# First stage of a hybrid decoder block: eighteen column tiles in the quarter passes instead of twelve, and three of eight modulation groups on VectorE

## The chip, the cores and the metric

One core of a Trainium2 chip runs the whole program. The metric is device microseconds per execution, the median of the runs shown. The engines are TensorE (PE, with its weight loads as PEld), VectorE (DVE), ScalarE (ACT), GpSimd (POOL) and SyncE (SP, which here only issues DMAs). Each works through its own instructions in the order in which they were written.

## The reference

A decoder block for 256 tokens of width 2048. Only its first part concerns the change:

```python
c_act = jax.nn.silu(c)
mod = jnp.einsum("bd,de->be", c_act, w_ada[l]) + b_ada[l]
shift1, scale1, gate1, shift2, scale2, gate2 = jnp.split(mod[:, None, :], 6, axis=-1)
h = rms_norm(x, norm1_g) * (1.0 + scale1) + shift1
proj = jnp.einsum("bsd,de->bse", h, w_in)      # 2048 -> 9248 columns
```

`proj` is cut into a gate branch and a recurrent branch (RG-LRU), and into the z, x, B, C and dt columns of an SSD (Mamba-2) branch with a causal convolution and a chunked scan. An output projection, a second normalization with modulation and a retrieval mixer (PEER) follow. All inputs are float32. The reference works in float32; the kernel splits each float32 weight and activation into a high and a low part and adds three products (high x high, high x low, low x high).

## The kernel before

**Column tiles.** `w_in` is stored as 73 column tiles of 128 columns, in the order `ETILES` names them: 0 to 15 are the LRU gate, 16 to 31 the LRU x, 32 to 47 z, 48 to 63 the SSD x, 64 to 67 B, 68 to 71 C, and 72 is dt. A tile's product with `hT` (the normalized, modulated input, 16 blocks of 128 rows, each with a high and a low part) ends in a PSUM bank, and `evac` takes it from there: for a convolved tile one ACT operation, three DVE taps, a tanh and two POOL or one DVE operation; for dt a softplus and two scans, a chain of some twenty small DVE operations spread over the following steps.

**Weight items.** Weights come in items of 512 KB through four `raw` buffers. ACT copies an item into the high part of an `hl` tile (L144, four of these), DVE subtracts it for the low part (L153), and then the next item's DMA is issued on SP.

**First stage.** The modulation of one quarter of `h`'s rows needs eight groups (`ada_group`), each of which reads 1 MB of `w_ada` (two `adw` tiles out of eleven): groups 0 to 3 of a quarter give the scale, 4 to 7 the shift. A group is four PE matmuls (L257) with the activated `c` as weights, four partial rows in one bank. After four groups `ada_row` copies the rows (ACT, L266), sums and turns them into columns on PE (L271) and finishes on DVE (L278, L280). Then ACT and DVE write that quarter of `hT` (L286, L288).

The eight groups of the first quarter run alone. Then come the passes 0, 1 and 2: in pass q, `w_pass` multiplies that quarter of the rows with each of the first twelve tiles, two tiles (a pair, 24 matmuls, L319 to L322) to an item, and the eight groups for the next quarter stand between the pairs. The sums of the six pairs stay in banks 0 to 5. Pass 3 has no groups; each tile goes to `evac` there. After each half of a pair or slot `mid` runs the steps that were put off (`defer`).

**Slots.** The other 61 tiles follow one by one in slots, two items each, 48 or 32 matmuls (L812 to L814, or the wide form in L444 and L446), into banks 0 to 2 in turn. Each slot also takes one step from the list `bg` (`bg_pop`): first an empty one, then the transposes of the dt results (L492, `cols_pe`), then for each of the four SSD groups the transposes of its x (L528, `a_pe`), the products of B and C, and so on. A group's steps are put on the list when its last x tile has been handed to `evac` (51 for the first group). `ada_step` accumulates the other modulation rows on DVE (L384), `ADA_SSD` of them per slot.

The order of the work is the order of the code; `manual_schedule` moves nothing.

Of the kernel before, what the change touches and what calls it, by code (L numbers as in the profile page):

```python
# [27 lines left out]
NRAW = 4  # L28
NHL = 4
GD = 3  # L30
ADA_SSD, ADA_LRU, ADA_OUT = 0.65, 1.1, 0.74

N0 = 12
NQ = 4
NG = 8
ETILES = [72]
for _g in range(4):
    ETILES += [64 + _g, 32 + 4 * _g, 68 + _g, 48 + 4 * _g, 33 + 4 * _g, 49 + 4 * _g, 50 + 4 * _g,
               34 + 4 * _g, 51 + 4 * _g, 35 + 4 * _g]
ETILES += [3, 16, 17, 18, 19, 20, 21, 22, 4, 5, 6, 7, 23]  # L40
for _g in range(2, 4):
    ETILES += [4 * _g + _i for _i in range(4)] + [16 + 4 * _g + _i for _i in range(4)]
for _n, _p in enumerate((3, 5, 7)):
    ETILES.insert(_p, _n)

KORDER = list(range(16, 32)) + list(range(16))

# [11 lines left out]
def hybrid_kernel(ctx, tc, xT, cols, w_ada, w_in, lru_w, w_o1, w_o2, w_q, keys, u_t, v_t, fng, out):  # L59
# [11 lines left out]
    def bank(n):  # L71
        return psum.tile([128, 512], FT, name=f"b{n}")
# [177 lines left out]
    def ada_group(n):  # L250
        q, r = divmod(n, 8)
        sec, c4 = divmod(r, 4)
        if c4 == 0:
            aw["b"] = bank(6 + sec)
        w = [ar.pop(2 * n + i) for i in range(2)]
        for g in range(4):
            pe.matmul(aw["b"][32 * g:32 * g + 32, :], cz[:, 4 * c4 + g, :], w[g // 2][:, g % 2],  # L257
                      start=(c4 == 0), stop=(c4 == 3), skip_group_check=True)
        for i in range(2):
            ada_load(2 * n + 11 + i)  # L260
        if c4 == 3:
            defer(lambda b=aw["b"]: ada_row(q, sec, b))

    def ada_row(q, sec, b):
        a = arow[:, sec]
        act.activation(a, b, AF.Copy)  # L266

        def cols_pe():
            p = bank(6 + sec)
            for i in range(4):  # L270
                pe.matmul(p[:, i:i + 1], a[:, i * 128:(i + 1) * 128], ones[:, 0:1], start=True, stop=True)  # L271
            defer(lambda: ada_fin(q, sec, p))
        defer(cols_pe)
# [33 lines left out]
    hT = keep.tile([128, 16, 2, 256], FR, name="H")  # L307
    b0 = {}

    def w_pass(q, n, done=None, late=False):  # L310
        w = take()
        for i in range(2):
            e = 2 * n + i
            if q == 0 and i == 0:
                b0[n] = bank(n)
            ps = b0[n][:, i * 256:(i + 1) * 256]
            for kk in range(4):
                k, c = 4 * q + kk, slice(i * 512 + kk * 128, i * 512 + (kk + 1) * 128)
                pe.matmul(ps, w[:, 0, c], hT[:, k, 0, :], start=(k == 0 and i == 0), stop=False,  # L319
                          skip_group_check=True)  # L320
                pe.matmul(ps, w[:, 0, c], hT[:, k, 1, :], start=False, stop=False, skip_group_check=True)
                pe.matmul(ps, w[:, 1, c], hT[:, k, 0, :], start=False, stop=(k == 15), skip_group_check=True)  # L322
# [20 lines left out]
    for q in range(3):
        for n, gs in enumerate(((0, 1), (2,), (3, 4), (5,), (6, 7))):
            w_pass(q, n)
            for g in gs:
                ada_group(8 * (q + 1) + g)
        mid()
        w_pass(q, n2 - 1, late=True)
# [169 lines left out]
    def ssd_steps(g):  # L519
# [117 lines left out]
        def seq(*fs):  # L637
            def go():
                for f in fs:
# [961 lines left out]
```

## Time and profile before

| | us |
|---|---|
| median of 3 runs (lowest to highest) | 2157.16 (2155.39 to 2159.13) |
| the profiled execution | 2172.81 |
| its span, first to last instruction | 2171.1 |
| PE busy / DVE / ACT / POOL | 2089.6 / 1397.3 / 960.7 / 879.2 |

An instruction's row gives its start in the span, its duration, engine, line, operation, and the tiles as out<-in; a bracket tells how long the engine was idle before it and what ended that. A row by line gives the busy time and the mean in ns. In rows by stage each engine's busy time is followed by its number of instructions. PE's matmuls overlap, so start to start tells more than a duration.

### The profile page before, as it was taken

Reading aid. Unit: us, or ns where it says so; the run is one execution under the profiler, and the core shown is the slowest. Engines: PE = TensorE matmul, PEld = TensorE weight load, DVE = VectorE, ACT = ScalarE, POOL = GpSimd, SP = SyncE. Lnnn points to the kernel's source line nnn. Section 1 sums busy time; section 2 is a strip of 40 time slices with the busy share of each in tenths; the row PEclk is TensorE's granted clock in tenths of the full one; section 3 lists DMA queues with packets and bytes.
Section 4 is the critical chain, followed back from the end, with each engine's and each line's share of the span. In section 5 each row is a group of like instructions: output and inputs, shape, how many; then the busy total and the mean of one; then the engine's idle time right before and its main releaser. Section 6 shows DMA issues by size and latency. Waiting matters only on the chain.

```text
span 2171.1 us, 34830 instructions
## 1 busy us (share of the span) xinstructions
PE 2089.6 (96%) x13092; PEld 1639.8 (76%) x13092; DVE 1397.3 (64%) x1996; ACT 960.7 (44%) x1470; POOL 879.2 (40%) x729
## 2 busy tenths in 40 slices
PE   7999999999999989999999999999999989999996
PEld 4779999978999888888788778666666656656663
DVE  2368887978878868879979996334334344344344
ACT  3346665666644454444345554333333333333332
POOL 0013233312212010001415561677777757767774
PEclk9999999999999999999999999999999999999998
DMA  9966566767789954568677778799999999999996
GB/s 372 387 233 223 195 207 216 235 224 251 262 295 322 334 176 166 191 220 282 229 255 238 247 247 288 270 367 346 347 343 354 347 325 346 373 345 348 358 356 234
DMA packets 248264, 616.33 MB, mean 284 GB/s; under 512 B 37752, under 2 KB 121864, under 8 KB 225800
## 3 DMA queue, kind: packets, MB, share of 16 engines
q1 hardware_dynamic: 188944, 387.73, 51.9%
q0 software_dynamic: 45056, 175.52, 21.9%
q10 hardware_dynamic: 14096, 50.86, 6.9%
q8 instruction: 103, 1.69, 0.3%
q14 instruction: 65, 0.53, 0.1%
HBM read 692.41 MB, written 14.69 MB: 326 GB/s over the span
## 4 chain that ended last, share of the span: by engine, by line
PE 70%; DVE 14%; DMA 9%; issue 4%; ACT 2%; POOL 0%; SPq 0%; another core or an unknown queue 0%; DVEq 0%; POOLq 0%; ACTq 0%
PE b L444 13%; PE b L1439 12%; PE b L1353 10%; PE b L446 7%; DVE hl L153 6%; PE b L1281 3%; PE b L1279 3%; PE b L1280 3%; PE b L918 3%; DMA raw<-in_w_in 2%; DMA two<-in_w_ada 2%; DMA adw<-in_w_ada 2%; PE b L812 2%; PE b L813 2%; PE b L814 2%
## 5 line engine op out<-in xcount | busy, mean ns | idle before, releaser
L144 ACT ACTIVATE hl<-raw 128x1024 fp32r<-128x1024 f32 x594 | 628.6, 1060 | 1072.2 <-PE b L1439 192.7
L153 DVE TENSOR_TENSOR hl<-raw,hl 128x1024 fp32r<-128x1024 f32 x594 | 766.5, 1301 | 140.2 <-ACT hl L144 121.0
L444 PE MATMUL b<-H,hl 128*128 128x512 f32 x1376 | 494.2, 402 | 3.2 <-DVE qT L450 2.8
L446 PE MATMUL b<-H,hl 128*128 128x256 f32 x1376 | 386.6, 281 | 5.2 <-DVE hl L153 5.1
L444 PEld LDWEIGHTS b<-H,hl 128*128 128x128 f32 x1376 | 259.1, 188 | 89.9 <-issue 20.2
L1332 POOL DMA_INDIRECT X<-ad,X x256 | 289.5, 1131 | 87.9 <-issue 76.8
L1439 PE MATMUL b<-hl,X 128*128 128x512 f32 x1152 | 279.0, 400 | 11.8 <-issue 10.0
L1439 PEld LDWEIGHTS b<-hl,X 128*128 128x128 f32 x1152 | 216.6, 191 | 87.0 <-issue 39.4
L446 PEld LDWEIGHTS b<-H,hl 128*128 128x128 f32 x1376 | 260.5, 189 | 7.4 <-DVE hl L153 6.6
L1281 PE MATMUL b<-hl,H 128*128 128x512 f32 x640 | 249.9, 390 | 4.0 <-DVE hl L153 3.7
L1279 PE MATMUL b<-hl,H 128*128 128x512 f32 x640 | 252.7, 395 | 0.0
L1280 PE MATMUL b<-hl,H 128*128 128x512 f32 x640 | 249.4, 390 | 0.0
L1323 POOL DMA_INDIRECT vq<-in_v_t,X x128 | 151.5, 1184 | 114.5 <-PE b L1353 38.1
L1323 POOL DMA_INDIRECT tk<-in_v_t,X x128 | 144.0, 1125 | 71.2 <-PE b L1353 31.4
L814 PE MATMUL b<-H,hl 128*128 128x256 f32 x560 | 160.0, 286 | 4.2 <-DVE hl L153 4.2
L1343 DVE TENSOR_TENSOR Wz<-X 128x4 f32<-128x4 f32 x64 | 11.0, 172 | 236.3 <-DMA X<-ad,X 123.0
L812 PE MATMUL b<-H,hl 128*128 128x256 f32 x560 | 162.4, 290 | 0.0
L813 PE MATMUL b<-H,hl 128*128 128x256 f32 x560 | 159.7, 285 | 0.0
L1281 PEld LDWEIGHTS b<-hl,H 128*128 128x128 f32 x640 | 120.1, 188 | 31.7 <-DVE hl L153 6.8
L384 DVE SCALAR_TENSOR_TENSOR adacc<-adr,cact,adacc 128x1024 f32<-128x1024 f32 x90 | 127.7, 1419 | 21.9 <-DMA adr<-in_w_ada 21.8
L1279 PEld LDWEIGHTS b<-hl,H 128*128 128x128 f32 x640 | 120.1, 188 | 23.9
L1280 PEld LDWEIGHTS b<-hl,H 128*128 128x128 f32 x640 | 120.3, 188 | 23.7
(323 smaller groups left out, 3212.2 us busy)
## 6 DMA issues: line engine op xcount, KB each, us to landing
raw<-in_u_t SPq DMA_DIRECT2D x208, 512.0 KB
raw<-in_w_in SPq DMA_DIRECT2D x146, 512.0 KB
adr<-in_w_ada SPq DMA_DIRECT2D x96, 512.0 KB
adw<-in_w_ada SPq DMA_DIRECT2D x64, 512.0 KB
raw<-in_w_o SPq DMA_DIRECT2D x64, 512.0 KB
raw<-in_u_t ACTq DMA_DIRECT2D x48, 512.0 KB
raw<-in_v_t SPq DMA_DIRECT2D x48, 512.0 KB
raw<-in_v_t ACTq DMA_DIRECT2D x48, 512.0 KB
```

Source lines behind the costliest of these rows:

```text
L144: act.activation(t[:, 0], r, AF.Copy)
L153: dve.tensor_sub(t[:, 1], r, t[:, 0].bitcast(FT))
L444: pe.matmul(ps, w[:, 0, c], x[:, k].rearrange("p a b -> p (a b)"), start=(k == 0), stop=False, skip_group_check=True)
L446: pe.matmul(ps[:, :256], w[:, 1, c], x[:, k, 0], start=False, stop=(k == 15), skip_group_check=True)
L812: pe.matmul(ps, wh, hT[:, k, 0, :], start=(k == 0), stop=False)
L1279: pe.matmul(o, hh, w[:, 0, :, kk], start=(k == 0), stop=False)
L1280: pe.matmul(o, hl_, w[:, 0, :, kk], start=False, stop=False)
L1281: pe.matmul(o, hh, w[:, 1, :, kk], start=False, stop=(k == 15))
L1323: pool.indirect_dma_start(x, None, vf, bass.IndirectOffsetOnAxis(ap=eV[:, t:t + 1], axis=0), bounds_check=E1 - 1, oob_is_err=False)
L1332: pool.indirect_dma_start(wA[:, n:n + 1], None, adf, bass.IndirectOffsetOnAxis(ap=eW[:, t:t + 1], axis=0), bounds_check=T * E1 - 1, oob_is ...
L1353: pe.matmul(sb[c][32 * g:32 * g + 32, :], Wz[:, x:x + 32], vs[4 * (q % 2) + g][:, c * 512:(c + 1) * 512], start=(m == 0), stop=(m == 31), ...
L1439: pe.matmul(ob[tb * 2 + c], w[:, i, s], v[:, k, c * 512:(c + 1) * 512], start=(jj == 0 and (i, k) == (0, 0)), stop=(jj == JD - 1 and k == 1))
```

## The change

The first eighteen tiles (nine pairs) are now computed in the passes. Pairs 0 to 5 keep banks 0 to 5. Pairs 6, 7 and 8 share bank 6 in turn; when one of them leaves the bank, its partial sum is copied (ACT) or added (DVE) into the first half of `xx`, which is free by then, and in pass 3 DVE adds it back to the bank before `evac` reads it (`first_evac`). Pass 0 holds eight pairs, pass 1 ten (pair 8 with two quarters), pass 2 nine, pass 3 nine. Of the eight groups of a quarter, 0, 4 and 5 run on DVE as four operations each into `arow`; the five others stay on PE, in bank 7, and DVE adds the two (L297 in the new file, in place of ACT's copy). In pass 3 `bg_pop` runs after each of the pairs 6, 7 and 8, and the empty first step of the SSD groups is left out except for the fourth. The order of the tiles behind the first twelve is rearranged, `y_ssd` (which takes `xx`'s place) is allocated later, and `ADA_SSD` is 0.86 instead of 0.65.

```diff
-ADA_SSD, ADA_LRU, ADA_OUT = 0.65, 1.1, 0.74
-N0 = 12
+ADA_SSD, ADA_LRU, ADA_OUT = 0.86, 1.1, 0.74
+N0 = 18
+NP = 6
+PASSES = [["P0", "G0", "G1", "P1", "G2", "P2", "G3", "P6", "P3", "G4", "P4", "G5", "G6", "P5", "G7", "P7"],
+          ["P0", "G0", "G1", "P6", "P1", "G2", "P2", "G3", "P8", "P8", "G4", "P3", "G5", "P4", "G6", "P5", "G7", "P7"],
+          ["P0", "G0", "G1", "P6", "P1", "G2", "P2", "G3", "P8", "P3", "G4", "P4", "G5", "G6", "P5", "G7", "P7"],
+          [f"P{_n}" for _n in range(N0 // 2)]]
...
+ADA_DVE = (0, 4, 5)
+ETILES = [72, 64, 32, 0, 68, 1, 48, 2, 33, 49, 50, 34, 51, 35, 3, 65, 36, 37, 69, 52, 38, 53, 54, 39, 55]
+for _g in range(2, 4):
...
     def ada_group(n):
...
-        if c4 == 0:
-            aw["b"] = bank(6 + sec)
...
-        for g in range(4):
-            pe.matmul(aw["b"][32 * g:32 * g + 32, :], cz[:, 4 * c4 + g, :], w[g // 2][:, g % 2],
-                      start=(c4 == 0), stop=(c4 == 3), skip_group_check=True)
+        if r in ADA_DVE:
+            a = arow[:, sec]
+            for g in range(4):
+                c, x = cact[:, 4 * c4 + g:4 * c4 + g + 1], w[g // 2][:, g % 2]
+                if c4 == 0 and g == 0:
+                    dve.tensor_scalar(a, x, c, None, op0=OP.mult)
+                else:
+                    dve.scalar_tensor_tensor(a, x, c, a, op0=OP.mult, op1=OP.add)
+        else:
+            first = r - 1 in ADA_DVE
+            if first:
+                aw["b"] = bank(7)
+            for g in range(4):
+                pe.matmul(aw["b"][32 * g:32 * g + 32, :], cz[:, 4 * c4 + g, :], w[g // 2][:, g % 2],
+                          start=first, stop=(c4 == 3), skip_group_check=True)
...
     def ada_row(q, sec, b):
         a = arow[:, sec]
-        act.activation(a, b, AF.Copy)
+        dve.tensor_add(a, b, a)
 
         def cols_pe():
-            p = bank(6 + sec)
+            p = bank(7)
...
+    def part(n):
+        j = 2 * (n - NP)
+        return xx[:, 0, j:j + 2, :].rearrange("p a b -> p (a b)")
+
-    def w_pass(q, n, done=None, late=False):
+    def w_pass(q, n, first, last, done=None, late=False):
         w = take()
+        if first:
+            b0[n] = bank(n if n < NP else n - NP if done else NP)
...
+        if last and not done:
+            def save(b=b, o=part(n), add=n in saved):
+                if add:
+                    dve.tensor_add(o, b, o)
+                else:
+                    act.activation(o, b, AF.Copy)
+            saved.add(n)
+            defer(save)
...
-        bg.extend([(None, None, 0), (a_pe, a_ew, 0),
+        if g == 3:
+            bg.append((None, None, 0))
+        bg.extend([(a_pe, a_ew, 0),
...
-    for n in range(n2):
-        w_pass(3, n, lambda e, ps: defer(lambda: evac(ETILES[e], ps)))
+
+    def first_evac(e, ps):
+        n, i = divmod(e, 2)
+        if n >= NP:
+            dve.tensor_add(ps, part(n)[:, i * 256:(i + 1) * 256], ps)
+        evac(ETILES[e], ps)
+    for q, n in passes[3]:
+        w_pass(q, n, n >= NP, True, lambda e, ps: defer(lambda: first_evac(e, ps)))
+        if n >= NP:
+            bg_pop()
...
-        ada["bank"] = 6 if slot >= 44 else (slot + 2) % 3
+        ada["bank"] = 6 if slot >= 38 else (slot + 2) % 3
```

The first of three places: DVE's order at the start, before and after. `xx` is the normalized input, `X` the row `arow`, `adw` a tile of `w_ada`. Before:

```order
L303 RECIPROCAL rstd_142<-rstd_142 128x256
L305 TENSOR_TENSOR xx<-xx,rstd_142 128x2048 x2
L278 TENSOR_TENSOR mod<-b_199,cc 128x4
L280 SCALAR_TENSOR_TENSOR mod<-mod,cc 128x4
L278 TENSOR_TENSOR mod<-b_237,cc 128x4
L288 SCALAR_TENSOR_TENSOR H<-xx,mod,H 128x256 x4
```

After:

```order
L334 RECIPROCAL rstd_142<-rstd_142 128x256
L336 TENSOR_TENSOR xx<-xx,rstd_142 128x2048 x2
L280 TENSOR_SCALAR X_95<-adw,cact 128x512
L282 SCALAR_TENSOR_TENSOR X_95<-adw,cact,X_95 128x512 x3
L297 TENSOR_TENSOR X_95<-b_156,X_95 128x512
L280 TENSOR_SCALAR X_95<-adw,cact 128x512
L282 SCALAR_TENSOR_TENSOR X_95<-adw,cact,X_95 128x512 x7
L309 TENSOR_TENSOR mod<-b_198,cc 128x4
L311 SCALAR_TENSOR_TENSOR mod<-mod,cc 128x4
L297 TENSOR_TENSOR X_95<-b_217,X_95 128x512
L309 TENSOR_TENSOR mod<-b_237,cc 128x4
L319 SCALAR_TENSOR_TENSOR H<-xx,mod,H 128x256 x4
```

Group 0's four operations and groups 4 and 5 now stand on DVE behind the two multiplications of `xx` and ahead of the scale's and the shift's last steps.

The second: DVE in pass 3, around the end of the dt chain (`dtt`, `acsr`) and the evacuation of tile 51. Before:

```order
L153 TENSOR_TENSOR hl<-raw,hl 128x1024
L482 TENSOR_TENSOR acsr<-dtt_1096,acsr 128x256
L421 SCALAR_TENSOR_TENSOR X_72<-b_492,hcw,X_72 128x255
L421 SCALAR_TENSOR_TENSOR X_72<-b_492,hcw,X_72 128x254
L421 SCALAR_TENSOR_TENSOR X_72<-b_492,hcw,X_72 128x253
L153 TENSOR_TENSOR hl<-raw,hl 128x1024
L486 TENSOR_TENSOR dtt_1097<-dtt_1097 128x128
L434 SCALAR_TENSOR_TENSOR X_72<-stmp,b_492 128x256
```

After:

```order
L531 TENSOR_TENSOR acsr<-dtt_1372,acsr 128x256
L470 SCALAR_TENSOR_TENSOR X_72<-b_514,hcw,X_72 128x255
L470 SCALAR_TENSOR_TENSOR X_72<-b_514,hcw,X_72 128x254
L470 SCALAR_TENSOR_TENSOR X_72<-b_514,hcw,X_72 128x253
L174 TENSOR_TENSOR hl<-raw,hl 128x1024
L535 TENSOR_TENSOR dtt_1373<-dtt_1373 128x128
L483 SCALAR_TENSOR_TENSOR X_72<-stmp,b_514 128x256
L851 TENSOR_TENSOR b_1581<-xx,b_1581 128x256
L470 SCALAR_TENSOR_TENSOR X_72<-b_1581,hcw,X_72 128x255
```

The chain's last operation (L486, now L535) had ten splits between the last quarter's H and itself and has nine; behind it, `b_1581` is the bank of pair 6, to which DVE adds the kept sum (L851) before tile 51's taps.

The third: PE around the transposes of dt (`dtt`) and of the first SSD group's x. Before, dt's stand between the second slot (bank `b_1376`) and the third:

```order
L444 MATMUL b_1376<-H,hl 128x512
L446 MATMUL b_1376<-H,hl 128x256
L492 MATMUL b_1425<-ident,dtt_1096 128x32 x2
L492 MATMUL b_1425<-ident,dtt_1097 128x32 x3
L812 MATMUL b_1431<-H,hl 128x256
```

After, between the pairs 7 (`b_1625`) and 8 (`b_1672`):

```order
L356 MATMUL b_1625<-H,hl 128x256
L357 MATMUL b_1625<-H,hl 128x256
L541 MATMUL b_1666<-ident,dtt_1372 128x32 x2
L541 MATMUL b_1666<-ident,dtt_1373 128x32 x3
L354 MATMUL b_1672<-H,hl 128x256
```

The x transposes stood between the fourth slot (`b_1502`) and the fifth:

```order
L444 MATMUL b_1502<-H,hl 128x512
L446 MATMUL b_1502<-H,hl 128x256
L528 MATMUL b_1552<-ident,X_72 128x128 x4
L528 MATMUL b_1557<-ident,X_72 128x128 x4
L812 MATMUL b_1562<-H,hl 128x256
```

and stand after the change between pair 8 and the first slot (`b_1725`):

```order
L356 MATMUL b_1672<-H,hl 128x256
L357 MATMUL b_1672<-H,hl 128x256
L577 MATMUL b_1715<-ident,X_72 128x128 x4
L577 MATMUL b_1720<-ident,X_72 128x128 x4
L872 MATMUL b_1725<-H,hl 128x256
```

Between pair 5 and dt's transposes stood two slots and now stand two pairs, which are half as long; up to x's it was four slots and is three pairs.

More of the change, by code (lines that the diff above doesn't have):

```diff
@@ L30, with pass_items @@
 GD = 3
-ADA_SSD, ADA_LRU, ADA_OUT = 0.65, 1.1, 0.74
-N0 = 12
+ADA_SSD, ADA_LRU, ADA_OUT = 0.86, 1.1, 0.74
[5 more added lines that the diff above has]
+          [f"P{_n}" for _n in range(N0 // 2)]]
+def pass_items():
+    done = [0] * (N0 // 2)
+    for p in PASSES:
+        o = []
+        for x in p:
+            n = int(x[1])
+            if x[0] == "P":
+                o.append((done[n], n))
+                done[n] += 1
+            else:
+                o.append((None, n))
+        yield o
 NQ = 4
 NG = 8
-ETILES = [72]
-for _g in range(4):
+ADA_DVE = (0, 4, 5)
+ETILES = [72, 64, 32, 0, 68, 1, 48, 2, 33, 49, 50, 34, 51, 35, 3, 65, 36, 37, 69, 52, 38, 53, 54, 39, 55]
+for _g in range(2, 4):
     ETILES += [64 + _g, 32 + 4 * _g, 68 + _g, 48 + 4 * _g, 33 + 4 * _g, 49 + 4 * _g, 50 + 4 * _g,
                34 + 4 * _g, 51 + 4 * _g, 35 + 4 * _g]
-ETILES += [3, 16, 17, 18, 19, 20, 21, 22, 4, 5, 6, 7, 23]
+ETILES += [16, 17, 18, 19, 20, 21, 22, 4, 5, 6, 7, 23]
 for _g in range(2, 4):
     ETILES += [4 * _g + _i for _i in range(4)] + [16 + 4 * _g + _i for _i in range(4)]
-for _n, _p in enumerate((3, 5, 7)):
-    ETILES.insert(_p, _n)
 KORDER = list(range(16, 32)) + list(range(16))
@@ L102, in hybrid_kernel @@
     items = []
-    for q in range(4):
-        for n in range(0, N0, 2):
-            items.append(w_in[n:n + 2, :, q * 512:(q + 1) * 512].rearrange("e p c -> p e c"))
+    for p in pass_items():
+        for q, n in p:
+            if q is not None:
+                items.append(w_in[2 * n:2 * n + 2, :, q * 512:(q + 1) * 512].rearrange("e p c -> p e c"))
     for n in range(N0, NE):
@@ L308, in hybrid_kernel @@
     b0 = {}
-    def w_pass(q, n, done=None, late=False):
+    def part(n):
+        j = 2 * (n - NP)
+        return xx[:, 0, j:j + 2, :].rearrange("p a b -> p (a b)")
+    def w_pass(q, n, first, last, done=None, late=False):
         w = take()
+        if first:
+            b0[n] = bank(n if n < NP else n - NP if done else NP)
+        b = b0[n]
         for i in range(2):
[L313 to L316, printed above, removed]
+            ps = b[:, i * 256:(i + 1) * 256]
             for kk in range(4):
                 k, c = 4 * q + kk, slice(i * 512 + kk * 128, i * 512 + (kk + 1) * 128)
-                pe.matmul(ps, w[:, 0, c], hT[:, k, 0, :], start=(k == 0 and i == 0), stop=False,
+                pe.matmul(ps, w[:, 0, c], hT[:, k, 0, :], start=(first and kk == 0 and i == 0), stop=False,
                           skip_group_check=True)
                 pe.matmul(ps, w[:, 0, c], hT[:, k, 1, :], start=False, stop=False, skip_group_check=True)
-                pe.matmul(ps, w[:, 1, c], hT[:, k, 0, :], start=False, stop=(k == 15), skip_group_check=True)
+                pe.matmul(ps, w[:, 1, c], hT[:, k, 0, :], start=False, stop=(last and kk == 3),
+                          skip_group_check=True)
             if i and not late:
@@ L326, in w_pass @@
             if done:
-                done(e, ps)
+                done(2 * n + i, ps)
+        if last and not done:
+            def save(b=b, o=part(n), add=n in saved):
+                if add:
+                    dve.tensor_add(o, b, o)
+                else:
+                    act.activation(o, b, AF.Copy)
+            saved.add(n)
+            defer(save)
         if late:
             issue_split()
-    n2 = N0 // 2
+    saved = set()
     for n in range(8):
@@ L342, in hybrid_kernel @@
         issue_split()
[L343 to L349, printed above, removed]
+    passes = list(pass_items())
+    for p in range(3):
+        for j, (q, n) in enumerate(passes[p]):
+            if q is None:
+                ada_group(8 * (p + 1) + n)
+            elif n < NP:
+                w_pass(q, n, q == 0, False)
+            else:
+                at = [x for x in passes[p] if x[0] is not None and x[1] == n]
+                if j == len(passes[p]) - 1:
+                    mid()
+                w_pass(q, n, (q, n) == at[0], (q, n) == at[-1], late=j == len(passes[p]) - 1)
         while any(stages):
@@ L620, in i_ew @@
         def i_ew():
+            nonlocal y_ssd
+            if y_ssd is None:
+                y_ssd = mix.tile([128, 16, 2, 256], FR, name="yssd", tag="Y1")
             sq = Z["sq"]
@@ L734, in evac @@
     def evac(e, ps):
-        nonlocal y_ssd
         if e == 72:
-            y_ssd = mix.tile([128, 16, 2, 256], FR, name="yssd", tag="Y1")
             S["BCs"] = mix.tile([128, 2, 2, 256], FT, name="BCs", tag=L[6])
```

## The prediction

> **What bounds the kernel now.** I read the page first, then the busy times by stage, then the order of time on TensorE (PE), VectorE (DVE) and the DMA queue around the change, then the waits.
>
> ```profile
> span 2171.1 us, 34830 instructions
> PE 2089.6 (96%) x13092; PEld 1639.8 (76%) x13092; DVE 1397.3 (64%) x1996; ACT 960.7 (44%) x1470; POOL 879.2 (40%) x729
> ```
>
> PE is busy nearly throughout, so work taken off it counts wherever PE is also what ends last. By stage (columns: PE, weight load, DVE, ACT, POOL, granted clock, DMA share, GB/s):
>
> ```profile
> 39.10:71.30 32.20, 30.04 (x219) 22.72 (x220) 7.95 (x11) 10.06 (x16) 0.00 (x0) 0.92 1.05 387
> 71.30:101.05 29.75, 29.19 (x230) 22.46 (x229) 9.28 (x14) 10.65 (x17) 0.00 (x0) 0.96 1.05 386
> 101.05:129.40 28.35, 28.02 (x227) 21.16 (x226) 9.27 (x14) 10.63 (x17) 0.00 (x0) 1.00 0.94 345
> 129.40:146.76 17.36, 17.36 (x146) 17.36 (x145) 16.94 (x31) 10.71 (x19) 2.07 (x3) 1.00 0.62 215
> 146.76:175.50 28.74, 25.05 (x174) 22.57 (x173) 27.85 (x46) 15.15 (x26) 9.63 (x10) 1.00 0.54 180
> 249.00:317.00 68.00, 66.85 (x499) 61.96 (x498) 60.74 (x96) 41.56 (x76) 22.48 (x19) 1.00 0.63 204
> ```
>
> The rows start where PE takes up passes 0, 1, 2 and 3 and the first slot. The first three are the passes 0 to 2: DMA at 386 GB/s and PE are both full, DVE is idle two thirds of the time. Rows four and five are pass 3 and the first slots: there DVE is the full engine (16.94 of 17.36, 27.85 of 28.74). The last row is one group of ten slots with its SSD steps: DVE at 89%. So the change adds DVE work where DVE is free, but sends PE into pass 3, where DVE is behind.
>
> **Parts that cancel.** Nine pair quarters (three pairs, three passes) move from the slots to the passes. A pair is 24 matmuls; the fourth row holds 144 in 17.36 us, 2.9 us a pair, so +26.0. Two slots run between these rows:
>
> ```profile
> 286.17 0.39 PE L812 MATMUL b<-H,hl 128*128 128x256 f32 x1
> ...
> 297.68 0.59 PE L612 MATMUL b<-sqv,ones 128*128 128x256 f32 x2
> ```
>
> That is 5.76 us a slot; six tiles lose three quarters of theirs: -25.9. Where both are bound by PE the move is worth nothing.
>
> **Groups off PE: -7.8.** A pass before has three places with two groups in a row and two with one:
>
> ```profile
> 104.11 1.92 PE L257 MATMUL b<-adw,cz 128*32 128x512 f32 x16
> 105.97 0.39 PE L319 MATMUL b<-H,hl 128*128 128x256 f32 x1
> ...
> 109.03 1.07 PE L257 MATMUL b<-adw,cz 128*32 128x512 f32 x8
> 110.02 0.38 PE L319 MATMUL b<-H,hl 128*128 128x256 f32 x1
> ```
>
> Two take 1.86 us from start to start, one 0.99: 3 x 1.86 + 2 x 0.99 = 7.56. After, five single ones remain, 4.95; -2.6 a pass, three passes. Their twelve DVE operations a pass, about 0.72 us each (half of L384 below), are 9 us in some 35 of a DVE with 9 us of other work: hidden.
>
> **The start: +4.0.** Group 0 moves behind the two multiplications L305 in DVE's order, and the queue on SP waits for it, since load 11 goes into group 0's first tile.
>
> ```profile
> 19.45 4.49 DVE L305 TENSOR_TENSOR xx<-xx,rstd 128x2048 f32<-128x2048 f32 x2
> 18.08 3.62 SPq L248 DMA_DIRECT2D adw<-in_w_ada  x6
> 22.42 5.09 SPq L136 DMA_DIRECT2D raw<-in_w_in  x4
> 27.89 0.37 SPq L248 DMA_DIRECT2D adw<-in_w_ada  x1
> 32.05 1.05 PE L257 MATMUL b<-adw,cz 128*32 128x512 f32 x4 [1.78 <-DMA adw<-in_w_ada]
> L384 DVE SCALAR_TENSOR_TENSOR adacc<-adr,cact,adacc 128x1024 f32<-128x1024 f32 x90 | 127.7, 1419 | 21.9 <-DMA adr<-in_w_ada 21.8
> ```
>
> Before, load 11 is issued at 18.08. After, DVE ends L305 at 23.94 and frees the first tile two operations later, at about 25.2. Loads follow each other every 1.37 us ((27.89 - 22.42) / 4). What was issued ahead, 8.1 MB at 387 GB/s from 2.2 us on, has landed by about 23.5, so the DMA engines run dry for 1.7 us, and load 11 then pays a whole latency. It lands near 29 instead of 25: all that follows is 4.0 late, and PE's last group of the first eight waits for such a load (32.05). Bounds: 1.7 (the dry time alone) and 7.1 (the issue's delay); 4.0 lies between, by latency.
>
> **Waits within the passes: -2.4.** Passes 0 to 2 take 90.3 us; three at the undisturbed 27.8 would take 83.3, so 7.0 are waits and half clock:
>
> ```profile
> PE b L271 <- ACT X L266: 3.0, 4, 1.7
> PE b L322 <- DVE hl L153: 1.8, 1, 1.8
> 36.30:43.10 6.80, 5.05 (x20) 4.52 (x21) 6.15 (x8) 3.93 (x6) 0.00 (x0) 0.50 1.05 387
> 70.40:73.80 3.40, 3.40 (x18) 3.40 (x18) 3.02 (x6) 1.54 (x4) 0.00 (x0) 0.50 1.05 387
> ```
>
> L271 will wait for DVE's sum (the new L297) instead of ACT's copy. In pass 0 the split of the fifth weight item stands ahead of that sum; its transfer, late by the 4.0, holds DVE and so PE for about 1.7. I add 0.4 at each of the five other sums and 1.0 of half clock: 4.6 in place of 7.0. Bounds: none left (-7.0), or 4 more than before. Sums kept in SBUF cost one 512-wide DVE or ACT operation per pass part, with two PE items before the bank is used again: nothing.
>
> **Pass 3: +7.9.** All times here count from DVE's first H operation of the last quarter.
>
> ```profile
> 128.85 1.69 DVE L288 SCALAR_TENSOR_TENSOR H<-xx,mod,H 128x256 fp32r<-128x256 f32 x4 [0.64 <-ACT H L286]
> 157.28 1.49 DVE L421 SCALAR_TENSOR_TENSOR X<-b,hcw,X 128x255 f32<-128x255 f32 x3
> 161.58 1.22 DVE L153 TENSOR_TENSOR hl<-raw,hl 128x1024 fp32r<-128x1024 f32 x1
> 162.72 0.28 DVE L486 TENSOR_TENSOR dtt<-dtt 128x128 f32<-128x128 f32 x1
> 162.74 0.56 PE L492 MATMUL b<-ident,dtt 32*128 32x32 f32 x5
> 174.75 1.03 PE L528 MATMUL b<-ident,X 128*128 128x128 f32 x8
> 163.41 1.65 POOL L432 TENSOR_TENSOR stmp<-stmp,X 128x256 f32<-128x256 f32 x1 [1.76 <-ACT stmp L429]
> 165.14 1.60 POOL L433 TENSOR_TENSOR X<-stmp,X 128x256 f32<-128x256 f32 x1
> PE b L446 <- DVE hl L153: 2.4, 2, 1.6
> PE b L814 <- DVE hl L153: 1.3, 1, 1.3
> ```
>
> DVE works without a break from H to L486, the last input of the dt transposes, which ends at 34.1. Before, PE arrives there (162.74) just then, having waited 3.7 on splits. After, DVE has the same list ahead of that operation with one split fewer: 34.1 - 1.1 = 33.0. But PE has only pairs P0 to P7 ahead of the transposes: 0.5 + 8 x 2.9 = 23.7, plus 1.3 for P7's split (the one that ends at 22.4). It stands from 25.0 to 33.0: 7.9. Then P8, until 36.5, and the transposes of x (now right behind P8, before four slots later). These need tile 51's add (0.4), ACT (0.6), three taps (1.5), tanh (0.4) and two POOL operations (1.7 to 3.3) behind the 33.0 and one 0.4 operation: 38.0 to 39.6, so 2.4 more. Together 11.6 against 3.7. Bounds: no wait at all (-3.7), and +10 if DVE comes 2 us later.
>
> After such a stall the clock may drop: the row at 70.40 shows 0.50 for 3.4 us after a wait of 1.7. The Trainium skill, "TensorE: Matmul & The Clock Gate", Part 1, says that an idle window of about 3.4 us halves the clock until a busy one has passed; the trace agrees in the length of the window (3.40). By that rule P8's 24 matmuls would take twice 2.9, an estimate of 2.2 to 2.9 more from this trace's pair; if tile 51 is late anyway that hides in its 2.4, and if not the result would be 2162.6 instead of 2160.4.
>
> **Behind it: +1.5.** The accumulation rate of 0.86 instead of 0.65 puts 0.21 x 1.42 = 0.3 us more DVE work into each slot, 3 us in a group of ten: DVE goes from 60.7 to 63.7 of 68. PE's waits on DVE there are
>
> ```profile
> PE b L666 <- ACT xct L417: 3.3, 1, 3.3
> PE b L446 <- DVE hl L153: 2.7, 1, 2.7
> PE b L814 <- DVE hl L153: 2.1, 2, 1.4
> PE b L592 <- DVE Dm L584: 1.1, 2, 0.8
> ```
>
> over 175 to 520 us. I take a sixth more, 1.5; bounds 0 and 5. The other moved steps (the y buffer taken later, one empty step ahead of the fourth group's SSD work, bank 6 from slot 38 on) keep their distance to the slots that they serve: nothing.
>
> **Sum.** +4.0 - 7.8 - 2.4 + 7.9 + 1.5 + 0.1 = +3.3. The profiled execution took 2172.81 (span 2171.1 and 1.7 around it), 15.6 above the median of 2157.16; I carry the difference over: 2176.1 there, 2160.4 as median. About 4.3 us, 0.2%, is what a measurement can tell from no change.
>
> **Rivals.** *PE is not held in pass 3 (faster).* If the dt chain reaches its last operation about when PE does, term five falls from +7.9 to -3.7: 2148.8. For it: only one chain of small DVE operations decides, and less elsewhere could pull it forward. Against it: DVE has no idle time in those two rows to give. It ends faster by 0.2% from a total wait below 4 us in pass 3.
> *DMA, not PE, sets the end of the passes.* By the instruction order the last w_ada load is transfer 94 instead of 87; 7 x 1.37 + 4.0 = 13.6 later, while the PE terms give 4.0 - 7.8 - 2.4 + 26.0 = 19.8. If PE has slack that I count as work, 6.2 go: 2154.2. For it: 386 GB/s without a gap. Against it: PE at 28.02 of 28.35 in pass 2.
> *VectorE sets the pace of the SSD slots (slower).* At 94% on average its lumps reach PE: 2 us for each of three groups and 1 behind, 7 instead of 1.5: 2165.9. For it: the waits above fall in the densest stretches. Against it: each slot has two buffered splits.
>
> **Chances.** Forecast 0.40 (own range 2156 to 2166), held nowhere 0.18, DMA 0.12, VectorE 0.30. The range 2150 to 2171 leaves out part of the first rival and the far ends of the start and the passes. Faster by over 0.2%: most of the first rival, a third of the DMA case, and a little: 0.23. Slower: most of the last, a quarter of the forecast: 0.38. Within: 0.39.
>
> **What would show it.** PE idle ahead of the five dt transposes (L541) of 6 to 9 us, released by DVE L535, and 1 to 4 ahead of L577. Load 11 issued near 25 us, and the first L357 matmul near 43 (before: 39.1, where the first row by stage starts). Pass 3 begins at 147 to 151. PE waits at L302 for DVE L297, the longest in pass 0. If pass 3 begins at 143 or earlier, or L541 waits under 2 us, the sum is wrong on the fast side; if DVE is over 97% busy through the slots and PE waits over 15 us on it there, on the slow side.

## The result: 1% slower, clear of the forecast

| | median us | lowest to highest | ratio to before, 95% interval |
|---|---|---|---|
| before, in the same session | 2156.27 | 2154.92 to 2159.13 | |
| changed | 2175.78 | 2174.58 to 2180.20 | 1.0097 [1.0082, 1.0112] |

The forecast was 2160.4 in a range of 2150 to 2171. By the ratio of the table 20.9 us were lost instead of 3.3 (the two medians differ by 19.5). The first lines of the page after the change:

```profile
span 2177.2 us, 34832 instructions
PE 2079.3 (96%) x13060; PEld 1648.8 (76%) x13060; DVE 1436.4 (66%) x2059; ACT 957.8 (44%) x1462; POOL 888.6 (41%) x729
```

PE is 10 us less busy than before, DVE 39 more. The spans differ by 6.1 us only, because the profiled execution of the kernel before lay 16.5 above its median, and an excess of that size sits behind the start of the query projection: from there to the end it took 1392.7 us, the changed kernel 1374.9. So the two are compared up to that point. Starts in us, read from the traces of the profiled executions:

| | first low-part matmul of pass 0 | DVE's H of the last quarter | first slot | output projection | query projection |
|---|---|---|---|---|---|
| before | 39.1 | 128.8 | 146.8 | 573.3 | 778.4 |
| changed | 44.7 | 153.9 | 196.5 | 598.3 | 802.3 |
| difference | +5.6 | +25.1 | | +25.0 | +23.9 |

The first slot isn't compared, since six tiles have changed sides of it. By stage (columns as in the prediction: PE, weight load, DVE, ACT, POOL, granted clock, DMA share, GB/s), passes 0 to 2, pass 3 with the transposes, and ten slots with their SSD steps:

```profile
44.71:80.63 35.92, 34.23 (x248) 28.76 (x248) 19.81 (x27) 11.65 (x17) 0.00 (x0) 0.91 1.05 387
80.63:119.34 38.71, 37.05 (x296) 31.79 (x296) 24.04 (x33) 14.70 (x21) 0.00 (x0) 1.00 1.05 386
119.34:154.47 35.13, 35.13 (x272) 30.27 (x273) 24.03 (x34) 13.01 (x18) 0.00 (x0) 0.95 0.77 279
154.47:196.51 42.04, 32.07 (x231) 30.88 (x230) 39.84 (x75) 21.52 (x40) 9.97 (x12) 0.85 0.44 152
265.00:334.00 69.00, 66.68 (x485) 61.74 (x484) 61.61 (x96) 40.91 (x77) 19.23 (x19) 0.98 0.61 199
```

The passes are as full as before. Pass 3 is the row that changed its nature: DVE is busy 39.84 of 42.04 us, PE only 32.07, and the granted clock is 0.85 on average where it was 1.00. PE's longest waits, first up to the first slot, then from there to the output projection (us in all, times, longest):

```profile
PE b L541 <- DVE dtt L535: 4.5, 1, 4.5
PE b L288 <- DVE mod L309: 4.1, 1, 4.1
PE b L357 <- DVE hl L174: 3.6, 2, 1.9
PE b L354 <- ACT H L317: 3.3, 2, 1.8
PE b L302 <- DVE X L297: 2.2, 2, 1.4
PE b L577 <- ACT scols L545: 2.2, 1, 2.2
PE b L541 <- DVE dtt L528: 1.4, 1, 1.4
```

```profile
PE b L442 <- DVE ggt L499: 9.1, 1, 9.1
PE b L577 <- POOL xs L482: 2.2, 1, 2.2
PE b L641 <- DVE Dm L633: 1.9, 1, 1.9
PE b L442 <- DVE xs L470: 1.7, 1, 1.7
```

The longest wait of the whole stage is one that no step of the prediction had. L442 is the column sum that ends a block of 16 accumulations; this one, the second, stands over 270 us behind pass 3. In order of time, PE, ACT and DVE around it:

```profile
469.91 0.28 PE L495 MATMUL b<-H,hl 128*128 128x256 f32 x1
479.24 0.99 PE L442 MATMUL b<-ones,adacc 128*128 128x1 f32 x4 [9.05 <-DVE ggt L499]
```

```profile
462.83 1.28 ACT L665 ACT_TABLE_LOAD   x1
...
464.61 1.28 ACT L740 ACT_TABLE_LOAD   x1
465.90 1.71 ACT L740 ACTIVATE X<-X,lspn 128x256 f32<-128x256 f32 x4
...
468.61 0.36 ACT L498 ACTIVATE ggt<-b 128x256 f32<-128x256 f32 x1
```

```profile
469.00 0.42 DVE L499 TENSOR_TENSOR ggt<-b,ggt 128x256 f32<-128x256 f32 x1 [6.91 <-ACT ggt L498]
...
471.14 1.75 DVE L666 RECIPROCAL rstd<-rstd 128x256 f32<-128x256 f32 x1
472.80 1.16 DVE L744 SCALAR_TENSOR_TENSOR X<-X,X 128x1024 f32<-128x1024 f32 x1
473.88 1.21 DVE L174 TENSOR_TENSOR hl<-raw,hl 128x1024 fp32r<-128x1024 f32 x1
475.01 3.75 DVE L684 SCALAR_TENSOR_TENSOR sqv<-yv,hsng,rstd 128x256 f32<-128x256 f32 x4
478.69 0.41 DVE L499 TENSOR_TENSOR ggt<-b,ggt 128x256 f32<-128x256 f32 x1
```

With the rate of 0.86 the second sum falls due in slot 37 (it was slot 44), one slot short of 38, from which on it gets bank 6. So it takes bank (37 + 2) % 3 = 0, in which a gate tile of slot 36 still lies. That tile leaves the bank with DVE's addition L499. DVE had waited 6.91 us for ACT (two table loads and the gates' ACT work ahead of L498) to do the L499 of the tile before; then it does an accumulation, a split, L666, L744, another split and L684 ahead of the L499 that PE needs (478.69). PE stands, and what follows in its order stands behind it, weights at hand or not. Behind the wait the records show 13.65 us at half clock (474.42 to 488.07), of which PE worked 8.83.

### The profile page after: what moved, and what is told of

Read it like the earlier page. It is cut to its first block, busy times and chain, and to the rows that moved or that the text cites. A ratio compares the mean times of both kernels' runs of the same rounds, so it can differ in the third digit from the quotient of the medians.

```text
span 2177.2 us, 34832 instructions
## 1 busy us (share of the span) xinstructions
PE 2079.3 (96%) x13060; PEld 1648.8 (76%) x13060; DVE 1436.4 (66%) x2059; ACT 957.8 (44%) x1462; POOL 888.6 (41%) x729
## 4 chain that ended last, share of the span: by engine, by line
PE 65%; DVE 18%; DMA 9%; issue 5%; ACT 2%; POOL 1%; SPq 0%; DVEq 0%; POOLq 0%; ACTq 0%
PE b L493 12%; PE b L1499 11%; PE b L1413 10%; DVE hl L174 7%; PE b L495 6%; PE b L1341 3%; PE b L1339 3%; PE b L1340 3%; DMA adr<-in_w_ada 2%; PE b L978 2%; PE b L872 2%; DMA two<-in_w_ada 2%; PE b L873 2%; PE b L874 2%; DMA raw<-in_w_in 1%
## 5 line engine op out<-in xcount | busy, mean ns | idle before, releaser
L493 PE MATMUL b<-H,hl 128*128 128x512 f32 x1312 | 471.2, 403 | 2.8 <-DVE qT L499 2.8
L495 PE MATMUL b<-H,hl 128*128 128x256 f32 x1312 | 367.9, 280 | 0.0
L493 PEld LDWEIGHTS b<-H,hl 128*128 128x128 f32 x1312 | 246.4, 188 | 88.2 <-issue 24.2
L1499 PE MATMUL b<-hl,X 128*128 128x512 f32 x1152 | 272.7, 394 | 6.0 <-ACT X L486 4.2
L495 PEld LDWEIGHTS b<-H,hl 128*128 128x128 f32 x1312 | 247.7, 189 | 0.3
L872 PE MATMUL b<-H,hl 128*128 128x256 f32 x528 | 155.3, 294 | 0.0
L874 PE MATMUL b<-H,hl 128*128 128x256 f32 x528 | 152.6, 289 | 0.8 <-DVE hl L174 0.8
L873 PE MATMUL b<-H,hl 128*128 128x256 f32 x528 | 152.7, 289 | 0.0
L433 DVE SCALAR_TENSOR_TENSOR adacc<-adr,cact,adacc 128x1024 f32<-128x1024 f32 x90 | 120.9, 1344 | 14.6 <-DMA adr<-in_w_ada 14.3
```

The source lines that it names most:

```text
L493: pe.matmul(ps, w[:, 0, c], x[:, k].rearrange("p a b -> p (a b)"), start=(k == 0), stop=False, skip_group_check=True)
L495: pe.matmul(ps[:, :256], w[:, 1, c], x[:, k, 0], start=False, stop=(k == 15), skip_group_check=True)
L872: pe.matmul(ps, wh, hT[:, k, 0, :], start=(k == 0), stop=False)
L1499: pe.matmul(ob[tb * 2 + c], w[:, i, s], v[:, k, c * 512:(c + 1) * 512], start=(jj == 0 and (i, k) == (0, 0)), stop=(jj == JD - 1 and k == 1))
```

## Experiments

Three chips were used. The runs of the bank, the start and the later transposes shared one, on which the kernel before took 2165.53 (19 runs); those of the groups, of fewer taps in the changed kernel and of the rate a second (2155.27, 13 runs); those of fewer taps in the kernel before and of the number of tiles a third (2155.60, 23 runs). Where times are compared across chips, it is by the ratio to the kernel before. Where one run is given, there is one measurement alone.

### The bank of one sum

```diff
-        ada["bank"] = 6 if slot >= 38 else (slot + 2) % 3
+        ada["bank"] = 6 if slot >= 37 else (slot + 2) % 3
```

> The changed kernel with one number different: the column sums of the accumulated modulation rows use bank 6 from slot 37 on instead of slot 38 on, so that the second of them, in slot 37, no longer writes the bank of the tile of slot 36. Theory 'bank': the 9.05 us wait at L442 (470 to 479 us) and the half clock behind it (13.65 us of 0.5, so some 6.8 lost) go: 2160 us (2157 to 2164), against 2175.8. Rival 'density' (the accumulation rate of 0.86 overloads VectorE, the place of the wait is chance): PE waits on VectorE a little later for as long, 2172 to 2177.

2182.86, ratio 1.0075 [1.0054, 1.0096]. The wait is gone (in that trace the sum's sixteen matmuls run from 465.9 us on and wait for nothing); in its place PE waits for splits, 4.4 us in all:

```profile
PE b L495 <- DVE hl L174: 4.4, 2, 2.6
```

The output projection starts at 588.3, 10.0 earlier than in the changed kernel, but 3.4 of these were there at the first slot already (193.1 against 196.5), ahead of the edit. From the first slot to the output projection it is 395.1 against 401.8, 6.7 us; by the ratios 4.7 us, with overlapping intervals. That is less than half of the 15.8 that were expected: by its ratio the time would be 2172.4 in the session of the result, in the range of the rival 'density'. Both theories hold in part. The place of the wait was the bank, but without it PE runs on into waits for VectorE at 477.47 (1.76) and 486.88 (2.64), about half as long. The mirror image makes the kernel before take a slot's bank for its sum in slot 44:

```diff
-        ada["bank"] = 6 if slot >= 44 else (slot + 2) % 3
+        ada["bank"] = 6 if slot >= 45 else (slot + 2) % 3
```

> The kernel before with the same number moved the other way: bank 6 from slot 45 on instead of 44, so that its second column sum, in slot 44, writes the bank of the tile of slot 43, a gate tile. Nothing else changes, the rate stays 0.65. Theory 'bank': PE waits there for VectorE's last read of that tile, 3 to 10 us with the half clock: 2160 to 2168. Rival 'density': no change, 2155 to 2158.

2172.15, ratio 1.0034 [1.0015, 1.0052], and the same wait appears in a kernel that has nothing else of the change; the output projection starts 5.3 later (578.6).

```profile
464.88 1.41 PE L393 MATMUL b<-ones,adacc 128*128 128x1 f32 x6 [7.20 <-DVE ggt L450]
```

One constant, one slot off: 5 to 7 us by traces and ratios, shown from both sides. By its ratio the mirror image costs 7.3, as the theory 'bank' expected and 'density' did not.

### The start

On top of the bank, the first quarter's groups all on PE again, in two banks, with ACT's copy:

```diff
-        if r in ADA_DVE:
+        if r in ADA_DVE and q:
...
```

> As e1_bank, and the eight groups of the first quarter all on PE again, as in the kernel before; the groups in the passes stay split. Theory 'start': pass 0 begins at 39 instead of 44.7 us and all that follows is earlier by about 5.6: 2154 to 2156. Rival 'absorbed' (the passes are bound by PE's or the DMA's own pace and take the delay up): 2159 to 2161, as e1_bank.

2174.79, ratio 1.0035 [1.0021, 1.0049]. Pass 0's mark is at 38.9 instead of 44.0 in the run above, and the 5.1 us stay: first slot 188.0 against 193.1, output projection 583.3 against 588.3. By the ratios it is 8.6.

### The groups and the pairs, apart

The kernel of the start with no group on DVE at all (two banks and ACT's copy in all quarters), so that only the pairs are moved:

```diff
-ADA_DVE = (0, 4, 5)
+ADA_DVE = ()
...
-        dve.tensor_add(a, b, a)
+        act.activation(a, b, AF.Copy)
...
```

> As e3_start_pe, but in the passes too all eight groups run on PE (sums in bank 7, ACT's copy instead of VectorE's sum); the eighteen tiles stay. Theory 'PE sets the passes': nine groups more on PE cost 7.8 us: the last quarter's H at 153 to 154 (145.8 in e3_start_pe), the output projection at 591, ratio to before some 0.36% above e3_start_pe's. Rival 'DMA sets the passes': H within 2 us of 145.8.

And the kernel before with nothing but groups 0, 4 and 5 of the later quarters on DVE (the four operations and DVE's sum as in the change):

```diff
+        if q and r in (0, 4, 5):
+            a = arow[:, sec]
+            for g in range(4):
...
```

> The kernel before with only one part of the change: groups 0, 4 and 5 of the three quarters that are loaded during the passes run on VectorE; twelve tiles, order, rate and the first quarter's groups as before. Theory: with twelve tiles DMA is already at 386 GB/s and PE loses 7.8 us of work that the DMA does not follow; the last w_ada load lands where it did, so H comes at 126 to 128 (128.8 before) and the time is 2 us shorter at most, ratio 0.998 to 1.000. Rival 'PE sets the passes here too': H at 121, ratio 0.996.

2169.46, ratio 1.0080 [1.0050, 1.0110], and 2152.67, ratio 0.9991 [0.9982, 1.0001]. The passes 0 to 2 in one row each: eighteen tiles with all groups on PE, eighteen with three on DVE (the kernel of the start), twelve with all on PE (before), twelve with three on DVE.

```profile
40.22:154.90 114.68, 112.74 (x887) 90.65 (x888) 39.43 (x50) 42.48 (x60) 0.00 (x0) 0.98 0.91 332
```

```profile
38.93:146.40 107.47, 104.94 (x815) 89.36 (x816) 67.65 (x92) 39.24 (x54) 0.00 (x0) 0.97 0.98 358
```

```profile
39.10:129.40 90.30, 87.26 (x671) 66.34 (x672) 26.50 (x37) 31.34 (x48) 0.00 (x0) 0.96 1.02 374
```

```profile
38.82:128.64 89.82, 82.32 (x599) 65.28 (x600) 54.74 (x79) 28.50 (x42) 0.00 (x0) 0.94 1.02 376
```

With eighteen tiles the groups take 7.8 us off busy PE and 7.2 off the passes. With twelve they take 4.9 off busy PE and 0.5 off the passes: there the DMA is full (share 1.02) and sets the end. In the kernel before a pass has 22 transfers of 1.37 us, 30.1, which is a third of 90.30. With eighteen tiles the passes have 75 such transfers, 102.8 us, and take 107.47, with PE busy 104.94: there PE sets the end.

### Pass 3

In the kernel with the bank mended, two of the three steps that the pairs of pass 3 take are put off (one behind the last pair only, one more in slot 1, no empty step ahead of the fourth group), so that PE meets the dt transposes later:

```diff
-        if g == 3:
-            bg.append((None, None, 0))
...
-        if n >= NP:
+        if n == N0 // 2 - 1:
             bg_pop()
...
         bg_pop()
+        if slot == 1:
+            bg_pop()
```

> As e1_bank, but the transposes of dt and of the first SSD group's x no longer stand among the pairs of pass 3: one step of the list is taken behind pair 8, the dt transposes come behind the first slot, the x transposes and the step after them both behind the second (and the empty step ahead of the fourth group's work is left out, so that it keeps its place). Theory 'VectorE behind': the evacuation of the 18 tiles on VectorE is what ends pass 3; without the transposes PE runs into the bank of pair 6, which VectorE has not emptied before about 38 us after the last quarter's H, so nearly nothing is gained: 2157 to 2161. Rival 'place': the transposes themselves cost the 5.9 and 2.2 us of waits and the half clock behind them: 2147 to 2152.

2180.97, ratio 1.0067 [1.0050, 1.0084], next to 1.0075 without the edit: no difference clear of the intervals. The waits at the transposes are gone, and PE stands as long one place further on, at the first slot, whose bank holds pair 6 until DVE has read tile 35:

```profile
189.73 0.58 PE L870 MATMUL b<-H,hl 128*128 128x256 f32 x1 [7.98 <-DVE X L483]
```

Counted from H the first slot comes 3.5 earlier in this trace, with the transposes now behind it, and the output projection 3.0. So most of the wait isn't the place of the transposes but VectorE's list of work. Taking work off that list (one tap of the convolution instead of three for the first seven convolved tiles; the two other taps are left out, and with them a part of the result):

```diff
+        npass[0] += 1
+        ds = (1, 2, 3) if npass[0] > 7 else (1,)
...
-            for d in (1, 2, 3):
+            for d in ds:
```

> As e3_start_pe, but the seven convolved tiles of pass 3 (64, 68, 48, 49, 50, 51, 65) get one of their three taps on VectorE; the two others are left out. Theory 'VectorE behind': five of these tiles stand ahead of the dt transposes, so VectorE comes there 10 x 0.48 = 4.8 us earlier, and by tile 51's another 1.0 at the first slot: PE's 2.9 + 4.3 us of waits at the dt transposes shrink to about 2.5, the first slot starts at 182 (188.0 in e3_start_pe) and the output projection at 577 (583.3). Rival 'chain' (the dt chain's own length, with its ACT steps, ends the wait): first slot at 186 to 188.

> The kernel before with one convolution tap instead of three for the same seven tiles as the run that did so on the changed kernel (its output differs by that): 14 DVE operations of 1.49 us less, 21 us of DVE work, by pass 3 and the first slots. If the change's loss in the slots is a debt of VectorE out of pass 3, the kernel before has little of it: PE loses at most the 3.7 us that it waits for splits up to slot 3, and the output projection starts at 569 to 572 (573.3 without the edit; the changed kernel gained 10.3 there by the same edit). If taps cost PE the same in both kernels, it starts near 563.

One run each: 2152.99 (the changed kernel with bank and start mended) and 2149.11 (the kernel before). In the changed kernel the first slot comes 5.7 earlier, at 182.3 as the theory 'VectorE behind' had it, and the output projection 10.3 earlier (573.0 against 583.3; 577 was expected); the kernel before gains 5.8 there (567.5 against 573.3). That is more than the 1 to 4 that were expected of it: waits for splits and half clock in its slots went too. (The second expectation counts 1.49 us for a tap; by the row it is the time of three, so fourteen taps are some 7 us, not 21.) The difference of the two gains is 4.5 us. It is the best figure here for what the changed kernel owes to pass 3 beyond the kernel before, but not an exact one: each side is one run, and in the kernel before two of the seven tiles belong to the slots.

### The slots

The old rate in the slots and a higher one in the output projection, in the kernel of the start:

```diff
-ADA_SSD, ADA_LRU, ADA_OUT = 0.86, 1.1, 0.74
+ADA_SSD, ADA_LRU, ADA_OUT = 0.65, 1.1, 0.84
```

> As e3_start_pe, with the rates of the accumulation on VectorE as 0.65 in the SSD slots instead of 0.86 and 0.84 instead of 0.74 in the output projection (its sums then fall into slots 27 and 42). Theory 'density': 0.3 us less VectorE work per slot takes away some 4 of the 17 us in which PE waits between the first slot and the output projection: that stretch takes 391 instead of 395.3. Rival 'structure' (the waits come from where the transposes, sums and evacuations now stand to each other): 394 to 396.

One run, 2173.52. The stretch from the first slot to the output projection, for the kernel before (57 tiles, from slot 4 on), the kernel of the start (55 tiles), and this one (55 tiles):

```profile
175.50:573.30 397.80, 386.67 (x2774) 358.27 (x2773) 333.60 (x426) 249.21 (x419) 112.38 (x86) 0.99 0.67 222
```

```profile
188.00:583.30 395.30, 378.40 (x2712) 349.92 (x2710) 328.65 (x421) 244.53 (x413) 113.69 (x87) 0.98 0.66 219
```

```profile
188.60:578.50 389.90, 374.55 (x2694) 345.89 (x2693) 321.10 (x412) 243.26 (x412) 108.92 (x87) 0.99 0.64 213
```

55 tiles at the pace of before would be 397.8 - 2 x 5.76 = 386.3; 395.3 are 9.0 more, of which the rate gives back 5.4. Not all of that is VectorE's load: with the rate the sums move too, and the first one, in slot 21, waits for a rotating bank like the second (L442 for VectorE's L470 above, 1.7; 1.64 in the kernel of the start, with 3.41 us at half clock behind it), while at the old rate it stands in slot 27 and PE doesn't wait ahead of it. The 5.4 isn't won: the accumulation is then behind its time, PE waits for it in the output projection, and the query projection starts at 796.3 instead of 786.1.

```profile
PE b L445 <- DVE adacc L436: 6.5, 2, 5.6
```

### How many tiles

If the DMA sets the end of a pass of twelve tiles and VectorE that of pass 3 with eighteen, the best number lies between. Fourteen tiles (pair 6 in bank 6 with its sum kept in SBUF, the groups on DVE behind the start, the old order and the old steps, rate 0.72, the sum's threshold at 42) and sixteen (pairs 6 and 7 share the bank, rate 0.76, threshold 40). For fourteen:

```diff
-ADA_SSD, ADA_LRU, ADA_OUT = 0.86, 1.1, 0.74
-N0 = 18
+ADA_SSD, ADA_LRU, ADA_OUT = 0.72, 1.1, 0.74
+N0 = 14
...
+PASSES = [list(_p) for _p in 3 * [["P0", "G0", "G1", "P1", "G2", "P2", "G3", "P3", "G4", "P4", "G5", "G6", "P5", "G7", "P6"]]] + [[f"P{_n}" for _n in range(N0 // 2)]]
...
-        ps = bank(slot % 3)
+        ps = bank((slot + 1) % 3)
...
-        ada["bank"] = 6 if slot >= 38 else (slot + 2) % 3
+        ada["bank"] = 6 if slot >= 42 else (slot + 3) % 3
```

> Fourteen tiles in the passes instead of eighteen: one pair more than before, groups 0, 4 and 5 on DVE in the passes and all on PE at the start, the old order of tiles, slots that take one step each, rate 0.72, the bank of the second sum out of reach of a gate's tile. If the passes are set by DMA, a pass is 23 transfers of 1.37 us, 31.5 instead of 30.1: pass 3 begins 4 us later (H at 132 to 133), lasts one pair longer, and two slots of 5.76 are gone: output projection at 568 to 570 against 573.3, time 0.1 to 0.25% under the kernel before. If VectorE has no room for a seventh pair in pass 3, PE waits at the dt transposes or behind them for 4 us or more and it starts at 573 or later: the same time as before.

> Sixteen tiles in the same manner (pairs 6 and 7 share a bank, their sums kept in SBUF), rate 0.76, no empty steps. By DMA alone: 24 transfers a pass, pass 3 begins 8 us later than before (H at 137), two pairs more in it, four slots fewer: output projection at 566 to 569, time 0.2 to 0.35% under the kernel before. By VectorE's debt: PE waits 4 to 8 us in pass 3 or on the banks of the first slots, and the slots lose 4 more: output projection at 573 to 578, no faster than before.

Fourteen: 2151.98, ratio 0.9986 [0.9974, 0.9999], the only version with the whole work whose interval lies below the kernel before, by 0.14% and barely. The groups alone, on another chip, gave 0.9991 (interval to 1.0001), so it isn't shown that the two further tiles bring anything on top of them. Sixteen: 2155.04, ratio 1.0009 [0.9995, 1.0023], no difference. DVE's H of the last quarter is at 131.8 and 137.2, as transfers of 1.37 us had it (132 to 133, 137). In both the output projection starts at 570.8, 2.5 earlier than before, where 568 to 570 and 566 to 569 were expected of the DMA alone. Two tiles more should bring 3.2 us (11.5 in slots, less 5.4 in the passes and 2.9 for the pair in pass 3), and PE's waits on splits take 3.8. The first two rows are these waits with fourteen tiles, 8.2 us; the others are PE's waits on VectorE with sixteen, of which L872, L497 and L359 are on splits, 12.0:

```profile
PE b L497 <- DVE hl L173: 4.2, 2, 2.8
PE b L874 <- DVE hl L173: 4.0, 3, 1.9
```

```profile
PE b L872 <- DVE hl L173: 7.4, 5, 2.8
PE b L930 <- DVE xct L472: 4.8, 1, 4.8
PE b L497 <- DVE hl L173: 2.7, 1, 2.7
PE b L643 <- DVE Dm L635: 2.6, 2, 2.1
PE b L359 <- DVE hl L173: 1.9, 1, 1.9
```

With sixteen PE also waits 4.8 for `xct` in the output projection, and at the query projection the two stand at 773.3 and 781.2.

## Why the prediction was wrong

Two terms of the sum failed: one that was put at nothing, and one, the largest gap, that was mis-sized.

**The step put at nothing** is the last line of "Behind it": that the moved steps, "bank 6 from slot 38 on" among them, keep their distance to the slots that they serve and cost nothing. The threshold was moved by six slots with the tiles, but the sum was moved by seven, from slot 44 to 37: two by the order of the tiles, five by the rate (at the old rate it falls in slot 42). Measured: a wait of 9.05, worth 5 to 7 us.

**The slots, +1.5, measured 9.0.** The mechanism was named (VectorE nearly full, its lumps reach PE), also as the rival "VectorE sets the pace of the SSD slots", which gave it 7; the size was taken a sixth above the waits before. Changing the rate back gives 5.4 of it in the traces. The averages don't show it: DVE is at 61.61 of 69.00 in the row of ten slots, 89% as before, and neither sign that was set for the slow side came. From the first slot to the output projection of the changed kernel DVE is busy 82%, and PE waits 13.4 us on it, the 9.05 included. In the kernel of the start PE's waits in that stretch are 16.8 against 11.0 before, and those that end with VectorE are 9.2 of them against 6.7; the others end with ScalarE, GpSimd or nothing that the trace shows, and whether they go back to VectorE isn't shown. Half clock cost 1.7 us more work. A further part may come out of pass 3, where VectorE ends behind; how much of the 9.0 that is alone, the runs don't settle, since fewer taps help the kernel before too.

**The start, +4.0, measured 5.1 by the edit that undoes it.** The queue went as forecast: load 11 is issued at 26.00 (25 was said), 7.9 later.

```profile
26.00 4.42 SPq L269 DMA_DIRECT2D adw<-in_w_ada  x6
```

```profile
34.37 1.08 PE L288 MATMUL b<-adw,cz 128*32 128x512 f32 x4 [4.11 <-DVE mod L309]
```

But PE's wait there ended with DVE, not with that load: the shift's groups use bank 7 too, whose scale columns DVE reads (L309) only behind the eight operations of groups 4 and 5. So the size was near, and the chain that I summed was not the one that ended last.

**The passes.** The pairs were near: with all groups on PE the last quarter begins 25.5 later (154.3 against 128.8; +26.0 was said), of which 1.1 is a later start; the passes themselves take 24.4 more. The groups were right, -7.8 busy and -7.2 in time, but only because of the pairs: with twelve tiles they are worth 0.5. The case of the rival "DMA sets the end of the passes" is therefore the kernel before and those with fourteen and sixteen tiles, while with eighteen PE does. The argument against it, PE at 28.02 of 28.35 in pass 2, didn't exclude it: the DMA share stood at 1.05 and 0.94 beside it. Without the start, the passes took 17.0 more (145.8 - 128.8) against 15.8 in the sum. PE's longest wait at L302 in the passes is in pass 0, as said, 1.45. The changed kernel's own execution began pass 3 at 154.5, outside the 147 to 151 that were said; with the bank mended alone H came 3.0 earlier, and what made that difference the runs don't settle. The 27.8 of an undisturbed pass, on which the term of -2.4 rests, stands in no row: PE is busy 28.02 in pass 2.

**Pass 3, +7.9.** The place and the cause were right, and the waits were near:

```profile
182.80 0.59 PE L541 MATMUL b<-ident,dtt 32*128 32x32 f32 x4 [1.44 <-DVE dtt L528]
187.85 0.31 PE L541 MATMUL b<-ident,dtt 32*128 32x32 f32 x1 [4.46 <-DVE dtt L535]
194.69 1.52 PE L577 MATMUL b<-ident,X 128*128 128x128 f32 x5 [2.16 <-ACT scols L545]
```

5.9 and 2.16, forecast 7.9 and 2.4, which rules out the rival "PE is not held in pass 3". Pass 3 still took 42.2 from H to the first slot with the start mended (188.0 - 145.8) against 39.6 by the prediction's times (36.5, a wait of 2.4 and 0.7 for the transposes of x). What was left out of the sum is the clock:

```profile
174.00:197.00 23.00, 13.03 (x70) 11.84 (x70) 21.29 (x43) 11.18 (x22) 6.95 (x8) 0.72 0.30 101
```

A mean of 0.72 over 23 us is 12.9 us at half clock, part of it under the waits. From H to the first slot PE worked 8.4 us at half clock, which is 4.2 us of work lost; with the start mended it worked 5.93 of 10.24 (174.92 to 185.16), 3.0 lost, about the 2.6 that are missing. The rule of the Trainium skill, "TensorE: Matmul & The Clock Gate", Part 1, which the prediction set aside as 2.2 for pair 8 alone, was on the right side.

**The sum.** With bank and start mended, +10.0 at the output projection instead of the sum's -0.7 there: +1.2 passes, +2.6 pass 3, +7.5 slots, which is 11.3 for the 10.7 between them (the pace of a slot, 5.76, is one measurement of two slots). Together with 5 for the start and 5 to 7 for the bank this makes 20 to 22; the ratio gives 20.9. The traces give 25.0 at the output projection: there the changed kernel's execution had lost 3.4 more ahead of the slots than the one with the bank mended, which no edit explains.

## What to carry to other kernels

Moving work between two stages is worth what the limits of the two differ by: look in each for what would set its end after the move (here DMA up to sixteen tiles, PE at eighteen, VectorE in the pass that evacuates them), and look for the optimum between them; here it was worth 0.14% at most. A constant that was tuned to an order of steps (a threshold in slots, a due time, a bank in turn) is part of every change that moves that order or a rate: work out in which slot each event falls, and whose buffer it takes there. A wait in front of an in-order engine may be ended by another operation than the one that you summed up, so list all that the engine does ahead of it.

## What the runs showed of the hardware

Waits much shorter than a window of the clock can be followed by one at half clock. In the changed kernel a wait of 1.45 us on PE ended at 62.53 and one of 1.53 at 118.82; the stretches behind:

```profile
64.82:68.23 3.41, 3.41 (x18) 3.41 (x17) 2.96 (x5) 0.00 (x0) 0.00 (x0) 0.50 1.05 384
119.43:122.84 3.41, 3.41 (x16) 3.41 (x17) 3.41 (x6) 1.60 (x3) 0.00 (x0) 0.50 1.05 387
```

Each such window costs 1.7 us of work, more than the wait before it. I had allowed 1.0 us for that in all three passes. The records show 98.4 us at half clock in the whole execution after the change and 61.5 before it; PE worked 65.3 and 45.1 of them, so 10.1 us more work were lost, as far as two single executions tell.

The changes of the clock lie on a grid of 3.413 us in each record, so one can ask how long PE must stand in a window of that grid for the next to be at half clock. Over all thirteen traces, from 45 to 770 us, with the column sums (matmuls one column wide) counted as standing: of 64 windows at full clock in which PE stood for 1.8 us or more, 62 were followed by one at half clock; of 2602 in which it stood for less, 4. With the column sums counted as work it is 43 of 45 and 23 of 2621, so they hardly seem to count as work. The wait of 1.45 us shows it: it is followed by 1.05 us of column sums (L302), and the window up to 64.82 has 2.04 us of both. The window up to 119.43, with 1.66 us, is one of the four. The Trainium skill, "TensorE: Matmul & The Clock Gate", Part 1, puts the drop behind an idle window of about 3.4 us, free-running; the length of the drop agrees (3.41), but in these traces a window that stood for a little over half, 1.8 us, was enough.
